# Queries, keys and most heads' probabilities turned by 32x32 block transposes and transfers instead of TensorE; softmax with a negative minimum, scaled on ScalarE

## The chip, the cores and the metric

One core of one Trainium2 chip. The time of a run is in device microseconds (us), that of the core from launch to end. A profiled execution gives a span, from the first to the last instruction, and the rows that are quoted here. The engines are PE (TensorE: matmuls and transposes by a matmul against an identity), ACT (ScalarE), DVE (VectorE), POOL (GpSimd) and SP (SyncE, which here only issues transfers). Each executes its own instructions in order and waits for the others by semaphores. PSUM is the memory into which PE writes; SBUF is the large on-chip memory.

## The reference

Two layers on x of 512 rows by 1024 columns. Layer 0 is retention with 4 heads, layer 1 chunked attention with 16 heads of 128; each has a gate, an output projection and a modulated RMS norm. The change is in layer 1:

```python
def chunked_attention_mixer(h, w_in, q_g, k_g, rel_table, w_out):
    q, k, v, g = jnp.split(h @ w_in, 4, axis=-1)               # each 512 x 2048
    q = rms_norm_f32(q.reshape(B, S, 16, 128), q_g)            # per head
    k = rms_norm_f32(k.reshape(B, S, 16, 128), k_g)
    ...
        s = jnp.einsum('bqhd,bkhd->bhqk', q_j, k_j) * scale + bias
        s = jnp.where(valid, s, jnp.float32(-1e30))
        p = jax.nn.softmax(s, axis=-1)
        return jnp.einsum('bhqk,bkhd->bqhd', p, v_j)
    ...
    o = o * jax.nn.silu(g.astype(jnp.float32))
    return o.astype(h.dtype) @ w_out
```

## The kernel before, in words

Every matmul operand is split into a high and a low part in a shorter format, and a product is three matmuls (high x high, high x low, low x high). A weight of 512 x 512 comes by one transfer on SP's queue into a "raw" tile; ACT copies the high part (`whi`), DVE subtracts to get the low part (`wlo`). There are two buffers of each. For the output projections POOL first multiplies the raw weight by the gate row (L219, `raw_a`).

Layer 1 runs from about 445 us. Its projections are chunks of 8 units of 12 matmuls of 128x512: two halves of the contraction, and in each half four units that accumulate into four PSUM buffers of pool `pm` (it has four). A unit's `evac` empties its buffer in the second half. There are 8 chunks of queries and keys (`aqk0` to `aqk7`, two heads each), 4 of values (`av`), 4 of the gate (`ag`) and 4 output projections (`po_a`). In `do_qk` a unit holds 128 rows of four heads' pieces a = 0..3 (two of queries, two of keys). `evac` squares each piece on ACT with a running sum (L659), POOL makes the mean and the reciprocal root (`ms`, `rs`, L117 and L119), and DVE multiplies the 128x512 unit by it (L663, `qn`). `turn` then transposes a piece by four matmuls into a buffer of PSUM pool `pa` (L671, `qt`), and ACT and DVE split it into the high and the low part (`qh`, `ql`, `kh`, `kl`; keys are scaled by `kq`).

A head h goes through `bias` (POOL fetches the bias tile `br` by a transfer and writes a corner by a memset behind its landing, L713 and L714; two buffers), four `softmax` steps i (three score matmuls `as`, a DVE pass that adds the bias and takes the row maximum, its negation `nm`, Exp on ACT with the row sum, reciprocal and scaling on DVE, in place in `p`), `turn` (ten transposes into `pt`, L745, split into `pth` and `ptl`), `mix` (matmuls with the values into `ao`) and `finish`. Tiles `p` and `qn` share a tag "p" of six buffers.

`hang` attaches these steps to units of the chunks: for loop n = 0..3 with heads 4n to 4n+3 the chunks are av, aqk(2n+1), aqk(2n+2), ag(n+1) and, in the first two loops, `po_a`; in the last loop they are av3, aqk7, po_a2 and po_a3. The numbers in `hang` say near which unit a step is emitted; a scheduler then writes the final order of every engine's queue at build time. That order, not the source's, is what runs.

## Time and profile before

| | us |
|---|---|
| median of three runs | 984.45 (982.43 to 985.0) |
| the profiled execution's own time | 982.98 |
| its span | 981.2 |
| PE busy in the span | 949.3 (97%) |
| DVE busy | 601.1 (61%) |
| ACT busy | 373.8 (38%) |
| POOL busy | 184.7 (19%) |

The time of the profiled execution is 1.8 us longer than its span, which is what lies before the first and after the last instruction. An engine's busy time is the sum over its instructions, in which overlapping ones count once. A matmul's row gives its time from start to end, and matmuls overlap: the pace of PE is read from the starts of successive rows. The granted TensorE clock is 0.992 of full speed over the span, and 1.00 in the stretches of layer 1 before 880 us.

### The profile page before, as it was taken

The page shows a single profiled execution, that of the slowest core. Times are in us where ns is not written, and L with a number is a line of the kernel's source. Part 1 is how long each engine was busy: PE and PEld are TensorE (multiplying, and loading weights), DVE is VectorE, ACT ScalarE, POOL GpSimd, SP SyncE. Part 2 cuts the span into 40 slices and gives each one's busy share as a digit, 9 for nine tenths or more (in the row PEclk, how much of TensorE's full clock was granted, in tenths as well). Part 3 has the DMA queues.
Part 4 walks back from the last instruction along what each step waited for, and adds up shares of the span by engine and source line. Part 5 has one row for each costly group of instructions (what it writes and reads, how often), then busy time and mean ns, then how long its engine had stood idle before and what let it go on. Part 6 is the DMA issues. An engine that isn't in the chain of part 4 may idle for free.

```text
span 981.2 us, 11783 instructions
## 1 busy us (share of the span) xinstructions
PE 949.3 (97%) x4528; PEld 793.6 (81%) x4528; DVE 601.1 (61%) x1023; ACT 373.8 (38%) x785; POOL 184.7 (19%) x169
## 2 busy tenths in 40 slices
PE   3889999999999999999999999999999999999997
PEld 2778888888888888778788888888878888888886
DVE  4977796568544775864455557444676346555674
ACT  6233322232233233354444445233543244444441
POOL 3000520051002012503001250002520012004410
PEclk8899999999999999999999999999999999999999
DMA  9654436434443433312333213223212232223202
GB/s 352 241 191 160 149 99 204 151 108 140 150 150 108 150 100 104 97 57 80 101 97 97 79 62 103 91 87 96 97 58 93 87 97 90 79 70 99 95 1 86
DMA packets 70296, 111.76 MB, mean 114 GB/s; under 512 B 11888, under 2 KB 36512, under 8 KB 70240
## 3 DMA queue, kind: packets, MB, share of 16 engines
q1 hardware_dynamic: 58256, 103.29, 31.5%
q0 software_dynamic: 10832, 5.62, 2.1%
q10 hardware_dynamic: 1152, 2.10, 0.6%
q8 instruction: 35, 0.57, 0.2%
q14 instruction: 21, 0.17, 0.1%
HBM read 108.83 MB, written 2.10 MB: 113 GB/s over the span
## 4 chain that ended last, share of the span: by engine, by line
PE 86%; DMA 4%; issue 4%; DVE 3%; ACT 1%; POOL 1%; SPq 0%; POOLq 0%; ACTq 0%; DVEq 0%
PE pm_aqk L233 5%; PE pm_aqk L231 5%; PE pm_aqk L232 5%; PE po_a L231 3%; PE po_a L233 3%; PE po_a L232 3%; PE pm_av L232 3%; PE pm_av L233 3%; PE pm_rg L239 3%; PE pm_rg L240 3%; PE ao L765 3%; PE as L725 3%; PE pm_av L231 3%; PE pm_rg L241 3%; PE ro L540 3%
## 5 line engine op out<-in xcount | busy, mean ns | idle before, releaser
L231 PE MATMUL pm_aqk<-whi_aqk,hTh 128*128 128x512 f32 x256 | 102.3, 400 | 1.1 <-ACT hTh L200 1.1
L233 PE MATMUL pm_aqk<-whi_aqk,hTl 128*128 128x512 f32 x256 | 100.4, 393 | 0.0
L232 PE MATMUL pm_aqk<-wlo_aqk,hTh 128*128 128x512 f32 x256 | 100.2, 391 | 0.0
L124 DVE CUSTOM_DVE_ANT_0 ada<-ada,cond 128x1024 f32<-128x1024 f32 x48 | 63.3, 1332 | 1.7 <-DMA ada<-in_ada_t_dram 1.7
L219 POOL TENSOR_TENSOR raw_r<-raw_r,gate 128x2048 f32<-128x2048 f32 x8 | 38.2, 4771 | 106.3 <-DMA raw_r<-in_ret_w_out_dram 92.9
L231 PE MATMUL pm_rv<-whi_rv,hTh 128*128 128x512 f32 x128 | 51.2, 407 | 6.7 <-ACT hTh L306 6.7
L231 PEld LDWEIGHTS pm_aqk<-whi_aqk,hTh 128*128 128x128 f32 x256 | 48.1, 188 | 10.9 <-ACT hTh L200 1.5
L233 PEld LDWEIGHTS pm_aqk<-whi_aqk,hTl 128*128 128x128 f32 x256 | 48.1, 188 | 10.6 <-DVE hTl L201 0.4
L232 PEld LDWEIGHTS pm_aqk<-wlo_aqk,hTh 128*128 128x128 f32 x256 | 48.2, 188 | 9.2
L734 ACT ACTIVATE p<-p,nm 128x128 f32<-128x128 f32 (+1 forms) x64 | 35.9, 563 | 48.7 <-DVE nm L732 47.6
L223 DVE TENSOR_TENSOR wlo_aqk<-raw_aqk,whi_aqk 128x2048 fp32r<-128x2048 f32 x16 | 36.6, 2290 | 28.0 <-ACT whi_aqk L222 28.0
L728 DVE CUSTOM_DVE_ANT_0 p<-as,br 128x128 f32<-128x128 f32 (+1 forms) x64 | 30.4, 486 | 36.9 <-PE as L725 34.0
L241 PE MATMUL pm_rqk<-hTh,wlo_rqk 128*128 128x512 f32 x128 | 49.7, 391 | 2.5 <-DVE wlo_rqk L223 2.5
L713 POOL DMA_DIRECT2D br<-in_att_bias_dram x16 | 13.4, 839 | 204.4 <-DVE nm L732 168.8
L232 PE MATMUL pm_rv<-wlo_rv,hTh 128*128 128x512 f32 x128 | 50.9, 402 | 0.0
L239 PE MATMUL pm_ag<-hTh,whi_ag 128*128 128x512 f32 x128 | 50.7, 397 | 0.0
L240 PE MATMUL pm_ag<-hTl,whi_ag 128*128 128x512 f32 x128 | 50.5, 394 | 0.0
L231 PE MATMUL po_r<-whi_r,yh 128*128 128x512 f32 x128 | 49.8, 391 | 0.5 <-ACT whi_r L222 0.5
L241 PE MATMUL pm_ag<-hTh,wlo_ag 128*128 128x512 f32 x128 | 50.2, 395 | 0.0
L233 PE MATMUL po_r<-whi_r,yl 128*128 128x512 f32 x128 | 50.1, 392 | 0.0
L232 PE MATMUL po_r<-wlo_r,yh 128*128 128x512 f32 x128 | 50.0, 391 | 0.0
L231 PE MATMUL pm_av<-whi_av,hTh 128*128 128x512 f32 x128 | 50.0, 391 | 0.0
(199 smaller groups left out, 2548.6 us busy)
## 6 DMA issues: line engine op xcount, KB each, us to landing
ada<-in_ada_t_dram SPq DMA_DIRECT2D x32, 512.0 KB, 4.4
raw_aqk<-in_att_w_in_dram SPq DMA_DIRECT2D x32, 512.0 KB, 4.6
ada<-in_ada_t_dram SPq DMA_DIRECT2D x8, 1024.0 KB, 13.8
raw_rg<-in_ret_w_in_dram SPq DMA_DIRECT2D x8, 1024.0 KB, 5.1
raw_r<-in_ret_w_out_dram SPq DMA_DIRECT2D x8, 1024.0 KB, 5.0
raw_ag<-in_att_w_in_dram SPq DMA_DIRECT2D x8, 1024.0 KB, 5.2
raw_av<-in_att_w_in_dram SPq DMA_DIRECT2D x8, 1024.0 KB, 5.1
raw_a<-in_att_w_out_dram SPq DMA_DIRECT2D x8, 1024.0 KB, 4.9
```

Of the source, the lines that this page charges most:

```text
L124: return nc.vector.tensor_tensor_reduce(raw, raw, cond, 1.0, 0.0, ALU.mult, ALU.add, mod[:, layer, block : block + 1])
L219: nc.gpsimd.tensor_tensor(raw, raw, scale.unsqueeze(1).broadcast_to([P, k1 - k0, width]), ALU.mult)
L223: nc.vector.tensor_tensor(lo, raw, f32(hi), ALU.subtract)
L231: nc.tensor.matmul(ps, a_h, wh[:, k, :], start=first and k == 0, stop=False)
L232: nc.tensor.matmul(ps, a_h, wl[:, k, :], start=False, stop=False)
L233: nc.tensor.matmul(ps, a_l, wh[:, k, :], start=False, stop=last and k == 3)
L239: nc.tensor.matmul(ps, wh[:, k, csl], h, start=first and k == 0, stop=False)
L240: nc.tensor.matmul(ps, wh[:, k, csl], l, start=False, stop=False)
L241: nc.tensor.matmul(ps, wl[:, k, csl], h, start=False, stop=last and k == 3)
L540: nc.tensor.matmul(ps[:, S - w :], a[:, fsl], b[:, psl], start=j == 0 and z == 0, stop=j == 3 and z == 2,)
L728: nc.vector.tensor_tensor_reduce(p[:, :w], ps[:, :w], br[:, S - w :], 1.0, -3.0e38, ALU.add, ALU.max, mx)
L734: nc.scalar.activation(p[:, :w], p[:, :w], AF.Exp, bias=nm, accum_out=sm)
```

## The change

Queries and keys: the unit is scaled by `rs` in four ACT copies out of PSUM instead of one DVE pass. DVE transposes it in blocks of 32x32 into `qx`. After the fourth unit `place` writes `qx` (1 MB) to a tile `mid` in DRAM and reads it back in four transfers of 256 KB, in runs of 512 bytes, so that the blocks land in the partitions where the full transpose wants them (`qt`, now in SBUF). The splits read `qt`; keys are scaled in place first. The 128 PE transposes are gone.

Probabilities: the DVE pass computes the negated sum and its minimum, which is the bias that Exp needs, so the negation goes. ACT scales by the reciprocal instead of DVE. For heads 0 to 13 DVE transposes blocks into `px`, whose unused part POOL clears by three memsets, and the same `place` brings them to `pt`; 140 of 160 PE transposes are gone. Heads 14 and 15 (`LATE`) keep theirs.

Room: tiles that layer 1 doesn't use move to a pool `lp` that is closed before it. In layer 1 the tag "p" has four buffers (six before) and "nat" three (four before). `turn` of a head is emitted at the earliest four units after its first softmax. All 22 places are issued on SP's queue, among the weight loads.

```diff
+    short = {"pool": lp, "p": 6, "nat": 4}
+    def short_tile(shape, tag, name, dt=F32):
+        return short["pool"].tile(shape, dt, tag=tag, name=name, bufs=short[tag])
...
+    lp_stack.close()
...
         ap = l1.enter_context(tc.tile_pool(name="ap", bufs=1))
+        short.update(pool=ap, p=4, nat=3)
+        dp = l1.enter_context(tc.tile_pool(name="dp", bufs=2, space=bass.MemoryType.DRAM))
+        def place(dst, src, name):
+            mid = dp.tile([P, 4, 4, P], F32, tag="mid", name=f"mid_{name}")
+            nc.sync.dma_start(mid, src.rearrange("p a c t i -> p a c (t i)"))
+            for c in range(4):
+                nc.sync.dma_start(
+                    dst[32 * c : 32 * c + 32].rearrange("j a (b x) -> j a b x", b=4),
+                    mid[:, :, c].rearrange("(b j) a x -> j a b x", j=32),
+                )
...
-                qn = np_.tile([P, 4, P], F32, tag="p", name=f"qn_{b}_{t}", bufs=6)
+                qn = short_tile([P, 4, P], "p", f"qn_{b}_{t}")
...
-                nc.vector.tensor_tensor(
-                    qn, ps4, rs.unsqueeze(2).broadcast_to([P, 4, P]), ALU.mult
-                )
-                nat.append(qn)
+                for a in range(4):
+                    nc.scalar.activation(qn[:, a, :], ps4[:, a, :], AF.Copy, scale=rs[:, a : a + 1])
+                nc.vector.transpose(qx[:, :, :, t, :], qn.rearrange("p a (c i) -> p a c i", i=32))
+                if t == 3:
+                    place(qt, qx, f"q{b}")
             def turn(a):
-                ps = pa.tile([P, 512], F32, tag="pa", name=f"qt_{b}_{a}")
-                for t in range(NT):
-                    nc.tensor.transpose(ps[:, t * P : (t + 1) * P], nat[t][:, a, :], ident)
+                src = qt[:, a, :].rearrange("p (b t i) -> p b t i", b=4, i=32)
...
+                if a >= 2:
+                    nc.scalar.activation(qt[:, a, :], qt[:, a, :], AF.Copy, scale=kq)
+                split(h4, l4, src)
...
             nc.vector.tensor_tensor_reduce(
-                p[:, :w], ps[:, :w], br[:, S - w :], 1.0, -3.0e38, ALU.add, ALU.max, mx
-            )
-            nm = sp.tile([P, 1], F32, tag="nm", name=f"nm_{h}_{i}")
-            nc.vector.tensor_scalar(nm, mx, -1.0, None, ALU.mult)
+                p[:, :w], ps[:, :w], br[:, S - w :], -1.0, 3.0e38, ALU.add, ALU.min, nm
+            )
...
-            nc.scalar.activation(p[:, :w], p[:, :w], AF.Exp, bias=nm, accum_out=sm)
+            nc.scalar.activation(p[:, :w], p[:, :w], AF.Exp, bias=nm, scale=-1.0, accum_out=sm)
...
-            nc.vector.tensor_scalar(p[:, :w], p[:, :w], ri, None, ALU.mult)
+            nc.scalar.activation(p[:, :w], p[:, :w], AF.Copy, scale=ri)
+            if h >= LATE:
+                pns[h, i] = p
+                return
+            if i == 0:
+                px = ap.tile([P, 4, 4, NT, 32], F32, tag="tx", name=f"px_{h}", bufs=2)
+                for j in range(1, NT):
+                    nc.gpsimd.memset(px[:, j, :, 0:j, :], 0.0)
+                pns[h] = px
+            nc.vector.transpose(
+                pns[h][:, : i + 1, :, i, :], p[:, :w].rearrange("p (j c i) -> p j c i", c=4, i=32)
+            )
+            if i == 3:
+                pt = ap.tile([P, 4, 512], F32, tag="tl", name=f"pt_{h}", bufs=2)
+                place(pt, pns[h], f"p{h}")
+                pns[h] = pt
...
-                at(b + (i + 1) // 2, turn, h, js)
+                at(max(b, a + 4 if h < LATE else 0) + (i + 1) // 2, turn, h, js)
```

The change also moves instructions. Three queues around query and key block 4 (loop n = 1; loops 0 and 2 read alike with heads 2 and 10 and blocks 2 and 6) show it. In a row, `out<-in` are the tiles with their buffer numbers; `as_6_0` are the scores of head 6, step 0, `pm_aqk4_3` is unit 3 of block 4, `pm_ag2_0` the first unit of the next gate chunk.

PE before: the scores of head 6 lie within block 4, whose second-half units follow and lie between them.

```order
L725 MATMUL as_6_0_5369<-kh_3_2_5352,qh_3_0_5343 128x256
L725 MATMUL as_6_1_5383<-kh_3_2_5352,qh_3_0_5343 128x256
L671 MATMUL qt_3_1_5397<-ident_92,qn_3_0_5183 128x128
L671 MATMUL qt_3_1_5397<-ident_92,qn_3_1_5213 128x128
L725 MATMUL as_6_0_5369<-kl_3_2_5353,qh_3_0_5343 128x256
L725 MATMUL as_6_0_5369<-kh_3_2_5352,ql_3_0_5344 128x256
...
L725 MATMUL as_6_2_5428<-kh_3_2_5352,qh_3_0_5343 128x384
L725 MATMUL as_6_2_5428<-kl_3_2_5353,qh_3_0_5343 128x384
```

PE after: all scores of head 6 and the first six score matmuls of head 7 stand behind the block's last matmul and directly ahead of the gate chunk.

```order
L240 MATMUL pm_aqk4_3_5410<-whi_aqk4_1_5457,hTl_1_3045 128x512
L747 MATMUL as_6_0_5371<-kh_3_2_5353,qh_3_0_5349 128x256
L747 MATMUL as_6_1_5388<-kh_3_2_5353,qh_3_0_5349 128x256
L747 MATMUL as_6_2_5423<-kh_3_2_5353,qh_3_0_5349 128x384
L747 MATMUL as_6_3_5436<-kh_3_2_5353,qh_3_0_5349 128x512
...
L747 MATMUL as_6_3_5436<-kl_3_2_5354,qh_3_0_5349 128x512
L747 MATMUL as_6_3_5436<-kh_3_2_5353,ql_3_0_5350 128x512
L747 MATMUL as_7_0_5588<-kh_3_3_5405,qh_3_1_5401 128x256
...
L747 MATMUL as_7_1_5605<-kh_3_3_5405,ql_3_1_5402 128x256
L246 MATMUL pm_ag2_0_5624<-hTh_1_3044,whi_ag2_0_5619 128x512
```

So the four units of block 4 fill the four `pm` buffers, and what lies between its last matmul and the first that needs one of these buffers is 18 score matmuls.

POOL before, at the same place: mean and root of block 4's first unit (`qss_4_0`) stand ahead of the bias transfer of head 8.

```order
L117 TENSOR_SCALAR ms_5481<-qss_4_0_5475 128x4
L119 TENSOR_TENSOR rs_5483<-ms_5481,mhalf_101 128x4
L713 DMA br_8_6003<-in_att_bias_dram 128x1x512
L117 TENSOR_SCALAR ms_5507<-qss_4_1_5501 128x4
L119 TENSOR_TENSOR rs_5509<-ms_5507,mhalf_101 128x4
L219 TENSOR_TENSOR raw_a1_0_5858<-raw_a1_0_5858,gate_1_110 128x2048
L117 TENSOR_SCALAR ms_5537<-qss_4_2_5531 128x4
L714 MEMSET br_8_6003 64x64
```

POOL after: behind the gate multiply of the output weight come the transfer and the memset of head 8's bias, and then that unit's mean and root.

```order
L226 TENSOR_TENSOR raw_a1_0_5843<-raw_a1_0_5843,gate_1_110 128x2048
L735 DMA br_8_5988<-in_att_bias_dram 128x1x512
L736 MEMSET br_8_5988 64x64
L124 TENSOR_SCALAR ms_5481<-qss_4_0_5475 128x4
L126 TENSOR_TENSOR rs_5483<-ms_5481,mhalf_101 128x4
L124 TENSOR_SCALAR ms_5511<-qss_4_1_5505 128x4
L226 TENSOR_TENSOR raw_a1_1_5906<-raw_a1_1_5906,gate_1_110 128x2048
L126 TENSOR_TENSOR rs_5513<-ms_5511,mhalf_101 128x4
L124 TENSOR_SCALAR ms_5538<-qss_4_2_5532 128x4
```

The memset now stands between the bias transfer and the first unit's root.

ACT after: the weight split of the gate chunk, the four Exps and the four scale steps of head 6 (first and last shown), the squares of all four units of block 4, and then the first unit's scaled copies.

```order
L229 ACTIVATE whi_ag2_1_5749<-raw_ag2_1_5748 128x2048
L755 ACTIVATE p_6_0_5375,sm_6_0_5378<-p_6_0_5375,nm_6_0_5376 128x128
...
L755 ACTIVATE p_6_3_5440,sm_6_3_5443<-p_6_3_5440,nm_6_3_5441 128x512
L758 ACTIVATE p_6_0_5375<-p_6_0_5375,ri_6_0_5380 128x128
...
L758 ACTIVATE p_6_3_5440<-p_6_3_5440,ri_6_3_5445 128x512
L682 ACTIVATE qn_4_0_5476,qss_4_0_5475<-pm_aqk4_0_5323 128x128 x4
L682 ACTIVATE qn_4_1_5506,qss_4_1_5505<-pm_aqk4_1_5336 128x128 x4
L682 ACTIVATE qn_4_2_5533,qss_4_2_5532<-pm_aqk4_2_5358 128x128 x4
L682 ACTIVATE qn_4_3_5562,qss_4_3_5561<-pm_aqk4_3_5410 128x128 x4
L687 ACTIVATE qn_4_0_5476<-pm_aqk4_0_5323,rs_5483 128x128 x4
```

Before, a DVE pass stood for the scaled copies, and the squares of the first unit stood ahead of the last two Exps of head 6.

## Rows read from the trace of the kernel before

**Rows 1.** Busy time by stretch: length, engines (instructions), clock, DMA share, GB/s
```profile
core 0: us, PE busy (x) PEld busy (x) DVE busy (x) ACT busy (x) POOL busy (x), PEclk, DMA share, GB/s
...
740.00:880.00 140.00, 140.00 (x683) 117.47 (x682) 75.99 (x160) 57.00 (x148) 14.66 (x24) 1.00 0.27 83
```

**Rows 2.** Waits of PE from 460 to 960 us: total, times, longest
```profile
PE pt L745 <- DVE p L737: 2.0, 2, 1.1
PE qt L671 <- DVE qn L663: 1.2, 1, 1.2
```

**Rows 3.** Groups by line on PE: busy us, mean ns | idle before, releaser
```profile
L745 PE MATMUL pt<-ident,p 128*128 128x128 f32 x160 | 27.3, 273 | 2.0 <-DVE p L737 2.0
L671 PE MATMUL qt<-ident,qn 128*128 128x128 f32 x128 | 18.7, 273 | 1.2 <-DVE qn L663 1.2
```

**Rows 4.** Timeline of PE at 666 us: start, length, line, operation
```profile
665.88 0.40 PE L233 MATMUL pm_aqk<-whi_aqk,hTl 128*128 128x512 f32 x1
666.12 0.82 PE L745 MATMUL pt<-ident,p 128*128 128x128 f32 x6
666.70 0.48 PE L231 MATMUL pm_aqk<-whi_aqk,hTh 128*128 128x512 f32 x1
667.01 0.40 PE L232 MATMUL pm_aqk<-wlo_aqk,hTh 128*128 128x512 f32 x1
```

**Rows 5.** Timeline of ACT from 435 to 465 us
```profile
435.23 1.48 ACT L198 ACTIVATE h<-hp,sh,gs 128x128 f32<-128x128 f32 x4
...
445.75 0.28 ACT L659 ACTIVATE qn<-pm_aqk 128x128 f32<-128x128 f32 x1 [0.72 <-PE pm_aqk L233]
...
446.67 0.22 ACT L659 ACTIVATION_READ_ACCUMULATOR qn<-pm_aqk 128x1 f32 x1
...
454.36 1.17 ACT L200 ACTIVATE hTh<-h 128x512 fp32r<-128x512 f32 x2
...
464.90 1.93 ACT L222 ACTIVATE whi_ag<-raw_ag 128x2048 fp32r<-128x2048 f32 x1
```

**Rows 6.** Groups by line on ACT
```profile
L734 ACT ACTIVATE p<-p,nm 128x128 f32<-128x128 f32 (+1 forms) x64 | 35.9, 563 | 48.7 <-DVE nm L732 47.6
...
L306 ACT ACTIVATE qh<-qt 128x512 fp32r<-128x512 f32 x16 | 9.6, 598 | 48.8 <-PE qt L671 42.7 <-issue 6.2
```

**Rows 7.** Groups by line on DVE
```profile
L663 DVE TENSOR_TENSOR qn<-pm_aqk,rs 128x512 f32<-128x512 f32 x32 | 22.0, 688 | 44.6 <-POOL rs L119 44.3
...
L223 DVE TENSOR_TENSOR wlo_ag<-raw_ag,whi_ag 128x2048 fp32r<-128x2048 f32 x8 | 18.3, 2290 | 4.2 <-ACT whi_ag L222 4.2
...
L728 DVE CUSTOM_DVE_ANT_0 p<-as,br 128x512 f32<-128x512 f32 x16 | 11.0, 685 | 2.7 <-PE pt L745 1.7 <-PE as L725 0.9
```

**Rows 8.** Timeline of PE at 574 us
```profile
573.78 0.28 PE L725 MATMUL as<-kh,qh 128*128 128x256 f32 x1
...
574.13 0.40 PE L239 MATMUL pm_ag<-hTh,whi_ag 128*128 128x512 f32 x1
```

**Rows 9.** Timeline of POOL from 660 to 699 us
```profile
660.15 0.79 POOL L713 DMA_DIRECT2D br<-in_att_bias_dram  x1 [43.97 <-DVE nm L732]
669.81 0.14 POOL L714 MEMSET br<- 64x64 f32 x1 [8.88 <-DMA br<-in_att_bias_dram]
...
670.32 1.04 POOL L119 TENSOR_TENSOR rs<-ms,mhalf 128x4 f32<-128x4 f32 x1
...
698.91 4.61 POOL L219 TENSOR_TENSOR raw_a<-raw_a,gate 128x2048 f32<-128x2048 f32 x1 [1.28 <-DMA raw_a<-in_att_w_out_dram]
```

**Rows 10.** DMA issues: queue, count, KB each, median us to landing
```profile
ada<-in_ada_t_dram SPq DMA_DIRECT2D x8, 1024.0 KB, 13.8
...
raw_ag<-in_att_w_in_dram SPq DMA_DIRECT2D x8, 1024.0 KB, 5.2
...
br<-in_att_bias_dram POOLq DMA_DIRECT2D x16, 256.0 KB, 8.3
```

**Rows 11.** Waits of SP's queue: total, times, longest
```profile
SPq L214 <- DVE wlo_aqk L223: 197.5, 15, 19.9
```

## The prediction

> **What bounds the kernel now.** I read the busy times by stretch first. In layer 1 TensorE (PE) is busy in all 140 us of the stretch from 740 to 880 us, while ScalarE (ACT) has 57.0 and VectorE (DVE) 76.0 [rows 1]: PE is the bound, and a change helps only by taking matmuls or waits off it. The waits of PE come second: on the lines that the change removes they are 2.0 us (two waits) and 1.2 us (one) [rows 2]. So almost nothing is to be gained from waits, and the gain is the PE time of the removed transposes. What can be lost is the fullness of PE: each new wait in front of a matmul is lost whole, since no other engine is the bound and none gives it back.

> **What the change removes from PE.** 128 transposes of queries and keys and 140 of the 160 of probabilities, 268. The groups by line give 273 ns for one [rows 3], but that runs from start to end of a pipelined instruction. The pace is what counts: at 666.12 six transposes stand in a row, and from there to the second next 512-wide matmul at 667.01 are 0.89 us, in which one 512-wide matmul lies; such a one takes 0.24 (665.88 to 666.12), so six take 0.65, or 0.11 us each [rows 4]. 268 x 0.11 = **-29.5 us**. Of the waits, the 1.2 is replaced below and about 0.9 of the 2.0 goes (the 1.1 stays with heads 14 and 15, which keep their transposes): **-0.9**.

> [...] The sum takes the 0.11.

> **What it adds off PE.** ACT: 128 scaled copies of 128x128 out of PSUM. The trace has none of this kind. From above, four 128x128 copies with scale and bias from PSUM take 1.48, 0.37 each; from below, four squares with their accumulator reads start at 445.75 and the last accumulator read at 446.67, about 0.28 each [rows 5]. That is 36 to 47 us. Add 64 scale steps of the probabilities at about 0.45 (a 512-wide copy takes 0.60 [rows 6], narrower ones less): 29, and 16 key scalings at 0.6: 10. Together 75 to 86 us over the 536 us of layer 1, 14 to 16 points on top of 41%: ACT does not become the bound by its load. DVE loses the multiplies (22.0 us) and the probability scaling and gets the block transposes, which I take at the price of a pass of the same width, 0.7 for 512 columns [rows 7]: about even. DMA: 22 places of 1 MB out and 1 MB back, 44 MB in 536 us, 82 GB/s on top of 83 at a share of 0.27 [rows 1]: room enough. None of these is a term. The terms are queues.

> **The narrow place, three times.** After the last matmul of query and key block 4 (and 2, and 6) PE now does the twelve score matmuls of head 6 (2, 10) and six of the next head, then the first matmul of the next g chunk. That one needs one of four PSUM buffers, which are all held by block 4 until ACT has made the four scaled copies of its first unit. Counted from the first score matmul:
> 1. PE's own work: six 256-wide at 0.117 (three between 573.78 and 574.13 [rows 8]), three 384-wide at about 0.175, three 512-wide at 0.24 = 1.95 us; six of the next head 0.7. PE arrives at **2.65**.
> 2. The last reduce of head 6 (0.69 [rows 7]) ends at about 2.8. POOL's bias transfer for head 8 waits for it, because the bias has two buffers and head 6 holds one, and POOL may still be in a 4.61 us gate multiply [rows 9]: issue at 2.9 to 4.0.
> 3. POOL's memset of that bias waits for the landing, 8.3 us by the median [rows 10], 9.66 from 660.15 to 669.81 [rows 9]: 11.2 to 13.7. Only behind it stand the mean and the rstd of block 4's first unit; from memset to end of rstd were 669.81 to 671.36, 1.55 [rows 9]: 12.8 to 15.2. In the kernel before these two stand ahead of the bias transfer.
> 4. Four scaled copies at 0.28 to 0.37: **13.9 to 16.7**. PE idles 11 to 14. I take **12**, nearest the median landing.

> ACT alone would not be much earlier. Its order is the weight split (1.92), four Exps (0.56 on average, 2.3 together [rows 6]), four scale steps (1.8; their reciprocals wait on DVE behind the 2.29 us weight remainder [rows 7]), sixteen squares (4 x 1.1), then the copies. The first square waits for the whole softmax of head 6, since the "p" tag now has four buffers and queries and probabilities share it. From 2.8: 2.3 + 1.8 + 4.4 + 1.1 = 12.4, idle **9.8**. That is the lower end, the upper 14.

> After it the second g unit waits for the second rstd, which stands behind another 4.61 us multiply: 24 matmuls (5.6) cover it but for 0.5, in two of the three loops: **+1**.

> **The other terms.** *Block 3's (1's, 5's) place.* PE has 96 matmuls x 0.24 [rows 4] and a head's mix of 1.9, about 25 us, from the block's last matmul to the first score that needs the result. The chain is eviction about 10 (POOL behind a bias landing again), 1 MB out and 1 MB back at 5.2 each [rows 10], five ACT passes of 0.6: 23.4, and up to 2.7 more behind a weight load on SP's queue, so 26 at the most by these rows. I take **+1** in each of three loops; the far end is the 13.8 us row for a megabyte [rows 10]. *Start of layer 1.* The first squares, at 445.75 now, have to wait for memory of the closed pool, that is behind the last copies at 454.36 + 1.17; the scaled copies then stand behind the weight split at 464.90 + 1.93 [rows 5], so a PSUM buffer is free at 466.8 + 1.2 = 468.0, where PE comes at 463.9. 4.2 less the 1.2 that went: **+3**. *Tail.* Softmax of heads 14 and 15 starts after the third output projection and not within it, with less PE work under it: **+3** (1 to 6, the length of a head's reduce, Exp and scale steps). *Output weights behind a place on SP's queue*: **+1**.

> **Sum.** 3 x (12 + 1) + 1 + 3 + 3 + 1 = +47, -29.5, -0.9: **+16.6** on the profiled execution's 982.98, 999.6. That execution lies 1.5 us under the median of 984.45, so against the runs I say **1000 us**.

> **Rivals.**
> *Faster.* The place is short and the 268 transposes win. It needs the idle time at each narrow place to stay under x with 3(x + 1) + 8 = 30.4, x = **6.5 us**. For it: PE's queue is long and ACT and POOL each have over half their time free. Against it: it takes both POOL's landing (8.3) out of the chain and the ACT chain down by a third. At 4 us a place: 983 - 30.4 + 15 + 8 = 976; with no narrow place at all, 983 - 30.4 + 3 + 8 = 964. 0.13.
> *The transposes are worth their listed time.* 268 x 0.273 = 73 us: 983 - 74 + 47 = 956. Rows 4 speak against it. 0.04.
> *Transfers late.* SP's queue now stops at 22 writes until they have landed, and weight loads stand behind them. Today SP waits for the weight buffers (197.5 us in 15 waits [rows 11]), so loads go out as soon as a buffer is free, and they have about 10 us to spare. If a 1 MB round trip takes 19 (5.2 out, 13.8 back) and not 10.4, three block places cost 8.6 more each: 1000 + 26 = 1026, and more where probabilities come late too. The read is in runs of 512 bytes, for which no row stands. 0.17.
> *A wash.* Idle time near 6.5 to 8 per place: 983 +- 3. 0.08.
> *The main case*, 1000, itself 990 to 1012 by the ends 9.8 and 14 of the place and 1 to 6 of the tail. 0.58.

> Within 0.3% is about 3 us here, the spread of the runs shown. Faster 0.17, same 0.08, slower 0.75. The range reaches to the nearer faster case and into the late transfers: 970 to 1025.

> **What would show it.** Right: in layer 1 PE's busy time falls by about 30 us while the span grows; three waits of 10 to 14 us on PE before the first matmul of a g chunk, released by ACT's scaled copy; POOL's mean and rstd directly behind a bias memset there; a wait of some 4 us at 464. Wrong: if those three waits are under 7 us, or if PE's waits name the weights or the splits of q, k and the probabilities with more than a few us each, then the transfers, and not the POOL and ACT queues, set the time.

## The result, and the profile after

The changed kernel takes 1094.81 us (median of 4 runs, 1094.12 to 1103.51), the kernel before 983.44 on the same chip: a ratio of 1.1154, 95% interval 1.1093 to 1.1214. The direction was forecast, the size was not: +111 us instead of +16.6, far above the range. The kernel before took 981.9 to 983.4 beside each of the runs below, so the runs may be compared with one another.

The page of the changed kernel (busy times, then the granted clock by fortieths of the span) and the stretch that answers to [rows 1]:

```profile
PE 954.5 (87%) x4260; PEld 785.6 (72%) x4260; DVE 606.6 (55%) x951; ACT 445.2 (41%) x993; POOL 187.9 (17%) x211
...
PEclk8999999999999999988998789998889998899899
```

```profile
740.00:880.00 140.00, 110.19 (x475) 89.86 (x474) 66.78 (x119) 59.15 (x146) 19.98 (x26) 0.89 0.47 134
```

The span is 1093.2 and PE's busy time 954.5, before 981.2 and 949.3. So PE idles 138.7 us and not 31.9: the 112.0 us are **106.8 of idle time and 5.2 of busy time**. That PE is busier although 268 transposes (29.5 us) have gone means 34.7 us that the sum didn't have. The clock row says where they are: in layer 1 fortieths at 7, 8 and 9 tenths, and 0.89 on average from 740 to 880 us, where [rows 1] have 1.00. Counted over the trace, 106 of the 2011 matmuls of 512 columns in layer 1 are followed by the next one only after 0.32 to 0.59 us and not after 0.23, which adds 19 us; narrower ones add 6.6 more. In the kernel before these sums are 1.6 and 1.5. So some 22 of the 34.7 us are slow matmuls; the rest isn't accounted for.

The waits of PE in layer 1 (total, times, longest); [rows 2] were 3.2 us:

```profile
PE pm_ag L246 <- ACT qn L687: 49.1, 5, 12.9
PE po_a L238 <- ACT whi_a L229: 12.9, 2, 6.8
PE ao L810 <- ACT pth L313: 11.7, 6, 4.0
PE as L747 <- DVE kl L314: 9.9, 3, 4.0
PE po_a L238 <- ACT qn L687: 7.8, 1, 7.8
PE as L747 <- ACT kh L313: 7.4, 3, 4.2
PE po_a L239 <- DVE wlo_a L230: 3.4, 3, 1.6
```

These are set against the sum of the prediction:

| term | in the sum, us | measured, us |
|---|---|---|
| narrow place, three loops | 36 | 38.4 (12.60, 12.85, 12.94) |
| start of layer 1 | 3 net | 9.8, less the 1.2 of before |
| second unit of the gate chunk | 1 | none in the three loops (0.8 at the start) |
| splits of q and k, waited for by scores | 3 | 17.3 (kl 9.9, kh 7.4), and 1.7 before scores with no releaser shown |
| output weights | 1 | 16.3 (12.9 and 3.4) |
| tail, a buffer for po_a | 3 | 7.8 |
| splits of the probabilities | 0 | 11.7 |
| slower matmuls | 0 | some 22 of the 34.7 above |

The narrow place came at about the size worked out. Here it is in the first loop (n = 0: block 2, heads 2 and 3, bias of head 4; start, length; in brackets the idle time before):

```profile
596.09 0.41 PE L747 MATMUL as<-kh,ql 128*128 128x256 f32 x1
609.10 0.80 PE L246 MATMUL pm_ag<-hTh,whi_ag 128*128 128x512 f32 x1 [12.60 <-ACT qn L687]
609.69 0.63 PE L247 MATMUL pm_ag<-hTl,whi_ag 128*128 128x512 f32 x1
610.12 0.63 PE L248 MATMUL pm_ag<-hTh,wlo_ag 128*128 128x512 f32 x1
...
613.00 0.39 PE L247 MATMUL pm_ag<-hTl,whi_ag 128*128 128x512 f32 x1
613.22 0.39 PE L248 MATMUL pm_ag<-hTh,wlo_ag 128*128 128x512 f32 x1
```

From the last score at 596.09 PE does nothing until 609.10. Behind the wait 512-wide matmuls start 0.43 us apart (609.69, 610.12), from 613.00 on 0.22: the granted clock is 0.50 of full from 597 to 609 and 0.60 on average from 609.1 to 613.1. It was at 0.50 already from 592.5, behind a wait of 4.00 us for `kl`. POOL and ACT at the same place:

```profile
587.38 4.52 POOL L226 TENSOR_TENSOR raw_a<-raw_a,gate 128x2048 f32<-128x2048 f32 x1 [20.46 <-DMA raw_a<-in_att_w_out_dram]
596.37 0.88 POOL L735 DMA_DIRECT2D br<-in_att_bias_dram  x1 [4.46 <-DVE nm L751]
606.33 0.14 POOL L736 MEMSET br<- 64x64 f32 x1 [9.08 <-DMA br<-in_att_bias_dram]
...
606.83 1.04 POOL L126 TENSOR_TENSOR rs<-ms,mhalf 128x4 f32<-128x4 f32 x1
```

```profile
596.00 0.72 ACT L755 ACTIVATE p<-p,nm 128x512 f32<-128x512 f32 x1 [0.28 <-DVE nm L751]
...
603.99 0.31 ACT L682 ACTIVATION_READ_ACCUMULATOR qn<-pm_aqk 128x1 f32 x1
607.90 1.14 ACT L687 ACTIVATE qn<-pm_aqk,rs 128x128 f32<-128x128 f32 x4 [3.61 <-POOL rs L126]
```

The steps of the prediction can be read off: last Exp 596.00 to 596.72, bias issued at 596.37 by the last reduce, memset at 606.33 behind the landing, mean and root right behind it, scaled copies at 607.90. ACT had finished its squares at 604.3 and waited 3.6 us for the root. Compare [rows 9]: there the same landing led to no wait of PE. The first score of this head is at 587.61. Counted from it, PE arrives at 8.9 us and not 2.65, and the buffer is free at 21.4 and not at 13.9 to 16.7: the wait for `kl` and the slow matmuls behind it moved both ends by some 6 us, and the difference held.

What the prediction hadn't got stands on SP's queue. A place of a head, and after it one of a query and key block:

```profile
601.02 0.34 SPq L663 DMA_DIRECT2D mid_p<-px  x1
610.56 2.61 SPq L665 DMA_DIRECT2D pt<-mid_p  x4
623.18 0.34 SPq L663 DMA_DIRECT2D mid_q<-qx  x1
627.01 2.60 SPq L665 DMA_DIRECT2D qt<-mid_q  x4
```

The write of head 2 takes from 601.02 until the reads are issued at 610.56, 9.5 us; the write of block 2, as large and laid out alike, 3.8 (623.18 to 627.01). The medians from issue to landing over all of them:

```profile
mid_p<-px SPq DMA_DIRECT2D x14, 1024.0 KB, 9.3
...
br<-in_att_bias_dram POOLq DMA_DIRECT2D x16, 256.0 KB, 9.8
```

A head's write is mostly issued 2 to 5 us after the bias of the head after next, since the same softmax releases both. The bias is 256 KB and lands after 9.8 us, 8.3 before [rows 10]: the two are under way together. The two writes of heads that were not under way with a bias for long, those of heads 11 and 13, landed after 3.8 and 4.3 us, the other twelve after 8.7 to 12.2. The writes of blocks 1, 3 and 5, each issued 0.6 to 1.2 us behind a weight load, took 7.6 to 8.1.

Reads can be late too. Two of the four reads of block 2's place landed after 10.4 and 10.7 us, beside the bias of head 5 and the write of head 3, where 3.4 to 5.8 is usual. ACT stands for them, and the weight split that the output projection needs stands behind:

```profile
639.80 0.63 ACT L313 ACTIVATE qh<-qt 128x512 fp32r<-128x512 f32 x1 [12.35 <-DMA qt<-mid_q]
...
642.08 1.90 ACT L229 ACTIVATE whi_a<-raw_a 128x2048 fp32r<-128x2048 f32 x1
```

The last part is DVE's. Two subtractions for the low part of the keys in the first loop (n = 0), and the same two in the third (n = 2):

```profile
587.59 5.47 DVE L314 TENSOR_TENSOR kl<-qt,kh 128x512 fp32r<-128x512 f32 x2 [0.44 <-ACT kh L313]
```

```profile
916.52 1.29 DVE L314 TENSOR_TENSOR kl<-qt,kh 128x512 fp32r<-128x512 f32 x2 [0.44 <-ACT kh L313]
```

5.47 us against 1.29. In the first loop POOL multiplies the output weight by the gate from 587.38 to 591.90 (first POOL row above); in the third there is no such multiply at that point, and no wait for kl. The multiply goes with two of the three waits for kl (4.00 and 3.86 us); beside the third, 2.01 us at 501, there is none.

### The profile page after: what moved, and what is told of

It is laid out like the page before. It is cut to its first block, busy times and chain, and to the rows that moved or that the text cites. A ratio compares the mean times of both kernels' runs of the same rounds, so it can differ in the third digit from the quotient of the medians.

```text
span 1093.2 us, 11654 instructions
## 1 busy us (share of the span) xinstructions
PE 954.5 (87%) x4260; PEld 785.6 (72%) x4260; DVE 606.6 (55%) x951; ACT 445.2 (41%) x993; POOL 187.9 (17%) x211
## 4 chain that ended last, share of the span: by engine, by line
PE 48%; DMA 24%; ACT 9%; DVE 9%; issue 4%; SPq 3%; POOL 3%; ACTq 0%; POOLq 0%; DVEq 0%
DMA mid_p<-px 5%; DMA qt<-mid_q 5%; DMA pt<-mid_p 5%; DMA br<-in_att_bias_dram 4%; DMA mid_q<-qx 4%; SPq L665 3%; PE pm_rg L247 3%; PE pm_rg L246 3%; PE pm_rg L248 3%; PE pm_rqk L248 3%; PE ro L547 3%; PE pm_rqk L246 2%; PE pm_rqk L247 2%; PE pm_rv L239 2%; PE pm_rv L238 2%
## 5 line engine op out<-in xcount | busy, mean ns | idle before, releaser
L238 PE MATMUL pm_aqk<-whi_aqk,hTh 128*128 128x512 f32 x256 | 99.8, 396 | 4.5 <-ACT qn L687 3.4
L246 PE MATMUL pm_ag<-hTh,whi_ag 128*128 128x512 f32 x128 | 53.3, 417 | 49.1 <-ACT qn L687 49.1
L688 DVE STREAM_TRANSPOSE qx<-qn 128x512 f32<-128x512 f32 x32 | 22.5, 707 | 84.1 <-ACT qn L687 83.9
L246 PEld LDWEIGHTS pm_ag<-hTh,whi_ag 128*128 128x128 f32 x128 | 25.7, 201 | 56.0 <-ACT qn L687 50.6
L687 ACT ACTIVATE qn<-pm_aqk,rs 128x128 f32<-128x128 f32 x128 | 36.1, 382 | 61.4 <-POOL rs L126 61.4
L238 PEld LDWEIGHTS pm_aqk<-whi_aqk,hTh 128*128 128x128 f32 x256 | 48.4, 189 | 16.3 <-ACT qn L687 5.2
L238 PE MATMUL po_a<-whi_a,yh 128*128 128x512 f32 x96 | 40.8, 425 | 21.1 <-ACT whi_a L229 12.9
L314 DVE TENSOR_TENSOR ptl<-pt,pth 128x512 fp32r<-128x512 f32 (+1 forms) x64 | 27.4, 486 | 54.2 <-ACT pth L313 54.2
L313 ACT ACTIVATE pth<-pt 128x512 fp32r<-128x512 f32 (+1 forms) x64 | 24.9, 458 | 77.3 <-DMA pt<-mid_p 74.4
L230 DVE TENSOR_TENSOR wlo_aqk<-raw_aqk,whi_aqk 128x2048 fp32r<-128x2048 f32 x16 | 36.7, 2291 | 28.9 <-ACT whi_aqk L229 28.9
```

The costliest lines, as they stand in the source:

```text
L230: nc.vector.tensor_tensor(lo, raw, f32(hi), ALU.subtract)
L238: nc.tensor.matmul(ps, a_h, wh[:, k, :], start=first and k == 0, stop=False)
L246: nc.tensor.matmul(ps, wh[:, k, csl], h, start=first and k == 0, stop=False)
L687: nc.scalar.activation(qn[:, a, :], ps4[:, a, :], AF.Copy, scale=rs[:, a : a + 1])
```

## The experiments

**Theory A**: the loss is waits of PE, each set by something off PE in its in-order queue (POOL behind the bias landing, the place behind the bias transfer, DVE behind POOL's multiply), and each followed by slow matmuls. **Rival B**: the work moved to ACT costs it. **Rival C**: each of the 22 places costs about the same. Ratios are to the kernel before on the same chip; times in us.

**No places at all** (`no_place`): `turn` of before, scaling still on ACT, LATE = 0, buffers as before.

```diff
-        short.update(pool=ap, p=4, nat=3)
+        short.update(pool=ap, p=6, nat=4)
-        LATE = AH - 2
+        LATE = 0
...
+                nat.append(qn)
+                ps = pa.tile([P, 512], F32, tag="pa", name=f"qt_{b}_{a}")
+                    nc.tensor.transpose(ps[:, t * P : (t + 1) * P], nat[t][:, a, :], ident)
```

> All 268 transposes are back on TensorE and nothing goes through DRAM; the negative minimum, the scaled copies and the probability scaling on ScalarE stay, with six p and four nat buffers as before. Theory A (the loss is waits behind the places' queues, behind the bias landing on GpSimd and behind the clock that falls after them): mean and root of the block's first unit stand ahead of the bias memset again and nothing waits for a transfer, so TensorE is full and the time is 980 to 995 us, no wait before a gate chunk over 2 us. Rival B (the work moved to ScalarE is what costs): 1020 us or more, with ScalarE named as releaser of TensorE's waits.

997.94, ratio 1.016 (1.0134 to 1.0187). Rival B's 1020 is excluded, but it is 3 us above A's range. Of PE's 13 us of waits 8.7 lie at the start, taken up below. The rest of the change, 97 us, comes with the places and what was done for them: the smaller pools (`p` 4, `nat` 3), the later `turn` and another order of the queues. No run has these without places.

**Only the probabilities, only queries and keys** (`only_p` and `only_q`).

```diff
-        short.update(pool=ap, p=4, nat=3)
+        short.update(pool=ap, p=6, nat=4)
...
+                ps = pa.tile([P, 512], F32, tag="pa", name=f"qt_{b}_{a}")
+                    nc.tensor.transpose(ps[:, t * P : (t + 1) * P], nat[t][:, a, :], ident)
...
-                px = ap.tile([P, 4, 4, NT, 32], F32, tag="tx", name=f"px_{h}", bufs=2)
+                px = ap.tile([P, 4, 4, NT, 32], F32, tag="tx", name=f"px_{h}", bufs=1)
```

> Queries and keys are transposed by TensorE again, still scaled by ScalarE; the probabilities of heads 0 to 13 keep their place. One px buffer and not two, six p and four nat buffers. Theory A: in this order only six score matmuls and no memset stand between block and gate chunk, so the narrow place's 12.8 us falls under 4, the start's 9.8 under 3, the key and query splits' 19 to nothing; the waits for pth (11.7 us) stay or grow. 14 us of transposes are back. 1000 to 1030 us. Rival C (each of the 22 transfers costs about the same, 112/22 = 5.1 us): 14 places cost 71, 1050 to 1060 us.

1048.11, ratio 1.0689 (1.0623 to 1.0756).

```profile
PE ao L811 <- ACT pth L313: 26.4, 11, 5.1
PE pm_ag L246 <- ACT qn L686: 16.2, 3, 6.6
```

A's size was wrong, 18 us above its range. The waits for pth more than doubled to 26.4, the gate chunks still wait 16.2 (6.6 at most) and the start 9.5. C's range is missed by 2 us. The single `px` buffer of this run is not tried by itself.

```diff
-        LATE = AH - 2
+        LATE = 0
```

> Probabilities are transposed by TensorE again in all heads, scaled by ScalarE; queries and keys keep their place. Four p and three nat buffers as in the changed kernel. Theory A: the bias memset still stands ahead of the block's mean and root, the score chain still ahead of its squares, so the narrow place keeps 8 to 13 us in each of three loops, now partly before the transposes of the probabilities, the start keeps 10 us, the splits 10 to 19; waits for pth are gone, the clock falls less often. 1040 to 1075 us. Rival C (loss by the number of transfers): 8 of 22 places, 41 us and 15 less gain, 1025 to 1035 us.

1067.20, ratio 1.0858 (1.0829 to 1.0888): A's range, well above C's, but not by A's waits:

```profile
PE ao L810 <- ACT pth L313: 13.1, 5, 4.1
PE pm_ag L246 <- ACT qn L687: 12.2, 5, 9.4
PE pt L790 <- ACT p L758: 10.8, 4, 3.5
```

The waits for pth stay although no head goes by place, and of the 12.2 before gate chunks 9.4 are the start: what is left of the narrow place is some 6 to 7 us in a loop, about half of it before the transposes of the probabilities, and not 8 to 13. Eight places cost more over no place (69 us) than fourteen (50), so the number of transfers alone is no measure, though this run also keeps the smaller pools, which `only_p` doesn't. Neither part alone explains the loss, and both together cost 97 over no place, less than their sum.

**The bias out of the way** (`bias_free`): the changed kernel, the corner written first, the transfer in groups of rows.

```diff
-            nc.gpsimd.dma_start(br, bass.AP(att_bias.tensor, h * 1280 + 127, [[576, 2], [-1, 64], [1, S]]))
-            nc.gpsimd.memset(br[0:64, 448:512], NEG)
+            a0 = h * 20480 + 127
+            nc.gpsimd.memset(br[0:64, 448:512], NEG)
+            nc.gpsimd.dma_start(br[0:64, 0:448], bass.AP(att_bias.tensor, a0, [[636, 16], [-1, 4], [1, 448]]))
+            nc.gpsimd.dma_start(br[64:128], bass.AP(att_bias.tensor, a0 + 16 * 636, [[636, 16], [-1, 4], [1, S]]))
```

> The changed kernel with one thing moved: the bias comes by two transfers that leave the masked corner out, spread over 16 groups of rows (the host repeats the rows 32 times and not twice), and the memset of the corner stands ahead of them and waits for no landing. [...] 1065 to 1080 us. Rival D (GpSimd is not in the chain and the ScalarE chain or the transfers set it): 1090 to 1097 us.

1042.47, ratio 1.0615 (1.0583 to 1.0646): 52 us off, more than A's 15 to 30 (1065 to 1080). A's estimate had about 9 us at the narrow place, a head's write falling from 9.3 towards the 3.8 of one that is alone, and half the waits for pth. The waits before the gate chunks are 9.19, 8.90 and 8.90, the predicted lower end of ACT's own chain; the write of a head lands after 4.9 and not 9.3, and pth is waited for 3.3 us and not 11.7. At the start of the layer PE waits 4.50 us and not 9.84, which A hadn't named. Two runs divide it.

**Spread, with the memset behind the landing** (`bias_wide`).

```diff
-            nc.gpsimd.dma_start(br, bass.AP(att_bias.tensor, h * 1280 + 127, [[576, 2], [-1, 64], [1, S]]))
+            nc.gpsimd.dma_start(br, bass.AP(att_bias.tensor, h * 10240 + 127, [[632, 16], [-1, 8], [1, S]]))
             nc.gpsimd.memset(br[0:64, 448:512], NEG)
```

> The changed kernel; the bias is one transfer again with the memset behind its landing, but spread over 16 groups of 8 rows (the host repeats the rows 16 times). Theory A: the landing takes 2.5 to 3.5 us and not 9.8; the root then comes about 7.5 us after the first score, ahead of the end of ScalarE's own chain, so the narrow place is 9 us as with the corner left out, and the place's writes take 5 us. 1035 to 1050 us, like the run before it. If the wait of the memset as such were the cost, 1060 us or more.

1039.46, ratio 1.0578 (1.0536 to 1.0619). Landings, PE's waits, and POOL at the start of the layer:

```profile
mid_p<-px SPq DMA_DIRECT2D x14, 1024.0 KB, 5.2
...
br<-in_att_bias_dram POOLq DMA_DIRECT2D x16, 256.0 KB, 3.2
```

```profile
PE pm_ag L246 <- ACT qn L687: 31.2, 4, 9.0
...
PE ao L810 <- ACT pth L313: 3.8, 1, 3.8
```

```profile
460.25 1.15 POOL L735 DMA_DIRECT2D br<-in_att_bias_dram  x2
```

The bias lands after 3.2 us and not 9.8. So it is the length of the landing, not that POOL waits for one. The two first bias transfers also go out back to back here, where the changed kernel has 7.60 us between them (below), and PE's wait at the start falls to 4.48: some 5 us of the gain are of this kind and not of the narrow place or the writes.

**Not spread, memset ahead** (`bias_slow`: the two transfers of `bias_free`, in 2 groups of 32 rows each; POOL waits for no landing).

```diff
-            nc.gpsimd.dma_start(br[0:64, 0:448], bass.AP(att_bias.tensor, a0, [[636, 16], [-1, 4], [1, 448]]))
+            nc.gpsimd.dma_start(br[0:64, 0:448], bass.AP(att_bias.tensor, a0, [[608, 2], [-1, 32], [1, 448]]))
```

> [...] Theory A: the narrow place falls to 9 us, 11 us in all; the places' writes stay at 8 to 9.5 us and with them the waits for pth and for the output weights: 1070 to 1085 us. Rival: the wait of GpSimd was all of it, 1035 to 1050 us.

1061.74, ratio 1.0791 (1.0751 to 1.083): between the two ranges and in neither, 8 us under A's.

```profile
mid_p<-px SPq DMA_DIRECT2D x14, 1024.0 KB, 7.6
...
br<-in_att_bias_dram POOLq DMA_DIRECT2D x16, 128.0 KB, 5.9
```

```profile
PE pm_ag L246 <- ACT qn L687: 36.1, 4, 9.3
PE ao L812 <- ACT pth L313: 13.6, 6, 3.8
```

The three narrow places wait as little as with the spread bias (9.3 at most), but the head's write takes 7.6 and pth is waited for 13.6. So about 33 of the 55 us (1095 to 1062) come with POOL's wait taken away and about 22 (1062 to 1039) with the spreading. The division is rough: in two halves the bias also lands sooner (5.9 and 4.7), and PE's wait at the start is 8.67 here and 4.48 with the spread bias, so that some 4 of the 22 are not the late writes. Why the grouping sets the landing no view here shows; measured are 9.8 us for 256 KB in 2 groups, 3.2 in 16, and 5.9 for 128 KB in 2.

**The descriptor space alone** (`scratch`: 4096 for the changed kernel, eight small tiles of layer 0 moved to `lp` for room; `no_place4k`: the same number in `no_place`, with every engine's order unchanged). In the changed kernel POOL stands between the two bias transfers at the start:

```profile
468.48 0.78 POOL L735 DMA_DIRECT2D br<-in_att_bias_dram  x1 [7.60 <-issue]
```

```diff
-        "TRN2", target_bir_lowering=False, num_devices=1, dynamic_dma_scratch_size=2048
+        "TRN2", target_bir_lowering=False, num_devices=1, dynamic_dma_scratch_size=4096
```

> The changed kernel with the descriptor space of GpSimd's transfers at 4096 as before and not 2048; eight small tiles of layer 0 move to the closed pool to make the room. The order of all queues around the places is the same. Theory A: at the start GpSimd stood 7.6 us between the first and the second bias transfer for want of that space; now they go out back to back, the first roots come some 8 us earlier, and TensorE's wait at the first gate chunk falls from 9.8 to about 5 us. 1087 to 1091 us. Rival: the 7.6 us are something else, 1093 to 1097 us and the wait stays.

1093.43, ratio 1.1113 (1.1075 to 1.115), no difference. The two transfers went out together (1.66 us for both) and the wait fell from 9.8 to 4.5, but with the moved tiles POOL's first memset of layer 1 stood at 466.77 and not at 459.66, so the time told nothing. In the second run every engine has the same instructions in the same order as in `no_place`:

> The kernel without places (998 us), with the descriptor space at 4096 and not 2048 and nothing else changed. Theory A: both bias transfers of the start go out in 1.7 us, the wait of 8.7 us before the first transposes falls under 2 us, 986 to 990 us. Rival: the wait belongs to ScalarE's queue, 996 to 1000 us.

991.98, ratio 1.0096 (1.0061 to 1.0132); the wait fell from 8.7 to 3.7. POOL without and with the space:

```profile
467.71 0.79 POOL L736 DMA_DIRECT2D br<-in_att_bias_dram  x1 [7.21 <-issue]
```

```profile
459.12 1.66 POOL L736 DMA_DIRECT2D br<-in_att_bias_dram  x2
```

That the descriptor space sets POOL's 7.21 us is shown, with every order the same. The size of the gain is about 6 us by the medians and not 8 to 12, since 3.7 of the wait stay, released by ACT; it is rough, since the four runs lie between 988.93 and 997.69 and the two intervals of the ratio hardly part.

**DVE beside POOL's multiply** (`no_gate`: `bias_wide` without the gate multiply of the first two output projections).

```diff
-                    [(ALLC, w_out[row0 : row0 + 512, csl])], f"{name}_{half}", scale=gate[:, csl],
+                    [(ALLC, w_out[row0 : row0 + 512, csl])], f"{name}_{half}", scale=None if name in ("a0", "a1") else gate[:, csl],
```

> The run with the bias in one spread transfer (1039 us), and GpSimd's gate multiply of the first two output projections' weights left out, so that part of the result lacks the gate. Theory A: DVE's second subtraction for the low part of the keys, 4.8 us instead of 0.69 while GpSimd multiplies, is held by that multiply; without it TensorE's waits for kl (7.8 us in two) fall under 1.5, and so does the clock's fall behind them: 1024 to 1033 us. Rival: DVE is late for another reason (the transfer, or its own queue) and the waits stay: 1036 to 1042 us.

1044.84, ratio 1.0641 (1.061 to 1.0673). The wait for kl is gone from the list, as A has it (all 16 of these subtractions in layer 1 now take 0.68 or 0.69 us), and that for the output weights falls from 4.8 to none. The time doesn't follow:

```profile
PE ao L810 <- ACT pth L313: 17.5, 3, 9.0
```

What was saved there is waited for at pth: 17.5 us against 3.8. The mixes of heads 3, 7 and 11 come before their place is back. A wait that is removed on PE is worth only what the next one leaves.

**The squares in a tile of their own** (`junk`: `bias_wide`, squares into one bf16 tile nobody reads, `qn` taken for the scaled copy).

```diff
-                        qn[:, a, :], ps4[:, a, :], AF.Square, accum_out=ss[:, a : a + 1]
+                        junk, ps4[:, a, :], AF.Square, accum_out=ss[:, a : a + 1]
```

> The run with the bias in one spread transfer (1039 us); the squares of queries and keys write into one small tile that nobody reads, and the p buffer is taken only for the scaled copy. The squares of block 4 then stand ahead of head 6's Exps. Theory A: the chain at the narrow place is last reduce 2.8, Exps 2.3, scale steps 1.8, block transpose 0.3, scaled copies 1.1, less 2.65 of TensorE's own work: 5.5 to 6.5 us of idle and not 8.9, three times: 1026 to 1033 us. Rival: the four buffers are not what holds it and it stays at 9, 1037 to 1042 us.

1064.18, ratio 1.0829 (1.0804 to 1.0854), above both ranges: the squares stood ahead of the Exps, yet the waits are 8.48, 10.09 and 6.81, and 23.1 came at pth. DVE's weight remainder, on which the reciprocals wait, took twice its time beside POOL's multiply; without that multiply (`junk_nogate`) it doesn't:

```profile
569.38 4.99 DVE L230 TENSOR_TENSOR wlo_ag<-raw_ag,whi_ag 128x2048 fp32r<-128x2048 f32 x1 [0.67 <-ACT whi_ag L229]
```

```profile
568.95 2.29 DVE L230 TENSOR_TENSOR wlo_ag<-raw_ag,whi_ag 128x2048 fp32r<-128x2048 f32 x1 [1.45 <-ACT whi_ag L229]
```

> The run with the squares in a tile of their own (1064 us), without the gate multiply of the first two output projections (part of the result lacks the gate). Theory A: DVE's weight remainder takes 2.3 us and not 4.99, the reciprocals behind it come 2.7 us earlier, and the waits before the gate chunks in the first two loops fall from 8.5 and 10.1 to 5.5 to 7 us; the third, without a multiply, stays at 6.8. 1050 to 1060 us in all, since the mix of the fourth head waits as before. Rival: the remainder stays near 5 us, 1062 to 1066 us.

1064.44, ratio 1.0829 (1.0803 to 1.0856), in the rival's range. The remainder takes 2.29 us and the waits are 7.59, 6.35 and 6.08, so A's mechanism holds for it, if not in size: the first is above its 7, and the third, which has no multiply and was to stay, fell as well. Again the time stays where it was: pth 22.4 and the gate tiles 9.7 take it back.

**Keeping PE busy in the wait** (`fill`, `fill50`: the changed kernel with 36 or 50 matmuls that nobody reads ahead of the later gate chunks).

```diff
+                ps = pa.tile([P, 512], F32, tag="pa", name=f"fill_{n}")
+                for r in range(50):
+                    nc.tensor.matmul(ps, hT["h"][:, 0, 0:P], hT["h"][:, 0, :], start=True, stop=True)
                 go(do_g(n + 1))
```

> The changed kernel with 36 matmuls of 512 columns that nobody reads ahead of each of the three later gate chunks, where TensorE idles 12.8 us. They take 8.5 us at 0.235 and up to 11 where the clock is still low. [...] Rival: the clock has nothing to do with idling, no change or the cost of the added work, 1094 to 1100 us.

1094.50, ratio 1.113 (1.1105 to 1.1156), no difference, where A's estimate was 1089 to 1092: 36 were too few. PE idle behind them and then the gate chunk (length, PE busy and instructions, granted clock, DMA share, GB/s):

```profile
602.50:606.90 4.40, 0.01 (x1) 1.00 0.46 194
606.90:611.00 4.10, 4.10 (x11) 0.58 0.29 83
```

4.4 us idle, and the clock, back at 1.00 before, is at 0.58 of full on average when the chunk starts.

> As the fill with 36 matmuls, which left 3.6 to 4.7 us idle in front of the gate chunks and the clock at its lower level behind them; 50 matmuls here, 3.3 us more at 0.235. [...]

1086.16, ratio 1.1052 (1.1028 to 1.1077), just inside A's estimate of 1086 to 1091, which had the clock full when the gate chunk starts. The same columns:

```profile
597.00:607.00 10.00, 10.00 (x45) 0.99 0.61 228
607.00:611.00 4.00, 4.00 (x20) 1.00 0.49 118
```

No idle time, full clock, gate matmuls from the first one 0.23 apart. (At the second place 2.34 us of idle time are left.) So idle time also costs in the matmuls behind it. With 150 matmuls more the kernel is about 9 us faster: the interval lies wholly below that of the changed kernel. But only part of this lies at the three places. From first to last matmul the gate chunks take 26.8, 26.6 and 26.5 us, in the changed kernel 28.9, 27.4 and 27.4, which is 3.9 us in all, and the stretches ahead of them give some 2 more. The rest of the 9.8 us between the two profiled executions is elsewhere, 2 us of it ahead of the first fill, where PE's order is the same and the wait for pth is 2.5 us and not 4.0.

**Two attempts at a kernel faster than both** (`cand1`: q and k wholly as before, 14 heads by place, bias as in `bias_free`; `cand4`: DVE scaling, 10 heads by place, bias as in `bias_wide`, descriptor space 4096).

```diff
+                nc.vector.tensor_tensor(
+                    qn, ps4, rs.unsqueeze(2).broadcast_to([P, 4, P]), ALU.mult
+                )
```

> Queries and keys wholly as before (DVE multiply, TensorE transposes), probabilities of heads 0 to 13 by place with the scaling on ScalarE, the bias in two spread transfers, six p, four nat and one px buffer. Theory A: the waits for pth were 26.4 us with the slow bias and fall with the writes' 4 us to about 10; the gate chunks' 16 us and the start's 9.5 us go, since DVE frees the first unit's buffer; 14 us of transposes are gone. 980 to 1000 us. If it comes under 980, the probabilities' half of the change pays once the bias is out of the way.

1009.84, ratio 1.0254 (1.022 to 1.0289), 10 us above A's range. PE still waits 16.7 us at the gate chunks, now for DVE's multiply (12.5) and its reciprocals (4.2), and 10.1 for pth.

```diff
-            if h >= LATE:
+            if not (h % 4 != 3 and h < 13):
...
-            nc.scalar.activation(p[:, :w], p[:, :w], AF.Copy, scale=ri)
+            nc.vector.tensor_scalar(p[:, :w], p[:, :w], ri, None, ALU.mult)
```

> Queries and keys wholly as before, all scaling of probabilities on DVE as before, six p and four nat buffers, descriptor space 4096; only heads 0, 1, 2, 4, 5, 6, 8, 9, 10 and 12 go by place, those whose mix did not wait in the run with 14 of them; bias in one spread transfer; negative minimum. 100 transposes less are 11 us. Theory A: no wait over 2 us is left on TensorE in layer 1, 972 to 980 us, faster than both kernels. Rival: the later turn and the reordered scores bring back waits of 10 us or more, 983 to 995 us.

997.31, ratio 1.0142 (1.0118 to 1.0165), above both ranges. Waits of up to 3.7 us, most of them for ptl, qn and pth and some 18 in all, are left where 11 us of transposes were gained. No version tried here beats the kernel before.

## Why the prediction was wrong

What held: the direction; PE as the bound (its idle time is 106.8 of the 112.0 us); the narrow place in place, releaser, steps and size (12.60 to 12.94 against 12, with both ends of it some 6 us late), and 9 us as the part that ACT's chain alone sets (9.8 given); that ACT's load is no bound (`no_place` 1.016). The amount of bytes is not what cost most either: `bias_wide` moves as many and is 55 us faster. The prediction's own sign of being wrong came true beside its signs of being right: PE's waits name the output weights (16.3), the splits of q and k (17.3) and of the probabilities (11.7).

What failed:
- **"None of these is a term. The terms are queues."** The transfers are a term. "Room enough" was read from the mean share of the engines, which says nothing of two transfers that are under way together. The bias in 2 groups of rows and a head's write beside it are both late: 9.8 and 9.3 us, against 3.2 and 5.2 with 16 groups. The chain for block 3 took 5.2 for a write and up to 2.7 for a neighbour, and the probabilities' places had no line in the sum at all. Measured: 11.7 us at pth, 16.3 at the output weights (ACT's weight split waits in its queue behind a place), falling to 3.8 and 8.8 when the bias was spread. The rival "transfers late" had the place of the loss and a round trip of 19 us, near the 17.3 of head 2, but gave it 26 us in all and the wrong half: the write is late beside the bias, while a read of 256 KB in runs of 512 bytes mostly lands within 5.8, late only beside other transfers.
- **"Block 3's place: +1 in each of three loops"** was 17.3 us, with block 0. 7.9 of them are DVE's subtraction beside POOL's multiply. Before, its source `qt` lay in PSUM, after in SBUF; that this was a change of the diff was not looked at. `no_gate`, without the multiply, has no wait for kl, and in the kernel before the subtractions took 0.68 and 0.74 us beside a multiply:

```profile
930.15 4.63 POOL L219 TENSOR_TENSOR raw_a<-raw_a,gate 128x2048 f32<-128x2048 f32 x1 [6.99 <-DVE x L324]
```

```profile
930.06 0.68 DVE L307 TENSOR_TENSOR ql<-qt,qh 128x512 fp32r<-128x512 f32 x1
930.65 0.74 DVE L680 SCALAR_TENSOR_TENSOR kl<-qt,kq,kh 128x512 fp32r<-128x512 f32 x1
```

The waits for kh, 0.9, 2.3 and 4.2 us, are nearer to the +1.
- **"Start of layer 1: +3"** was 8.6. The prediction has ACT's weight split as the last to end; in the trace it ends at 465.71, and ACT then stands 5.25 us for POOL's root, which is late because POOL stood 7.60 us between the bias transfers. The halved descriptor space was in the change and has no word in the prediction; `no_place4k` and `scratch` show 5 us of the wait.
- **No term for the clock.** PE's busy time was to fall by 29.5 and rose by 5.2. That idle time slows what follows could be read in the kernel before, though not in layer 1, which has no such wait. In layer 0 PE idles 2.63 us and, behind eight transposes, 4.01 us more; the granted clock is 0.50 from 20 to 25 us, and the matmuls behind are 0.43 apart:

```profile
23.42 0.80 PE L231 MATMUL pm_rv<-whi_rv,hTh 128*128 128x512 f32 x1 [4.01 <-ACT hTh L306]
24.01 0.63 PE L232 MATMUL pm_rv<-wlo_rv,hTh 128*128 128x512 f32 x1
24.44 0.63 PE L231 MATMUL pm_rv<-whi_rv,hTh 128*128 128x512 f32 x1
```

In the changed kernel the slow matmuls are some 22 us, as counted above; `fill50` shows about 4 of them in three gate chunks. What the other 12 of the 34.7 are stays open.
- **"Tail: +3"** was 7.8, a fourth narrow place: block 7's units hold the buffers that po_a2 needs, and ACT stands 13.6 us for POOL's root behind the landing of the last bias (11.1 us). With the spread bias this wait is gone. The narrow place was looked for only in the three loops that have an ag chunk.

What stays open: the terms don't add. Taking waits away moved the time by more than was forecast (`bias_free`) or by none (`junk_nogate`; in `no_gate` it is 5 us longer, with intervals that overlap), with what the scheduler made of the order in each. What the smaller pools and the new order cost without the places was not tried. The ledger above says where PE stood, not what each cause alone is worth.

## What to carry to other kernels

Here, on an engine that was full, a 0.11 us transpose in the stream was cheap, and the detour through DRAM cost a chain of five queues; look at each queue for what stands behind its waiting instruction, and at the diff's small numbers (buffers, descriptor space, an operand that moves from PSUM to SBUF) as closely as at its main idea. Ask of each added transfer which other transfer its own trigger also releases, and in how many groups of rows that one goes. Look in the kernel before for what TensorE's idle time does to the matmuls behind it (in these runs waits of 4 to 13 us had matmuls at half their pace behind them), put that into the sum beside the wait itself, and expect a removed wait to show up at the next place.
